# Output projection of an HGRN2 encoder layer by Strassen's seven products instead of eight

## The chip, the cores and the metric

The kernel runs on one core of one Trainium2 chip. The metric is the device time of one execution in microseconds (us). The core has five engines that run their own instruction rows side by side: PE (TensorE, matrix products; its weight loads are shown apart as PEld), DVE (VectorE), ACT (ScalarE), POOL (GpSimd) and SP (SyncE), which here does nothing but issue DMA transfers, in the order of its row. An engine works its row off in order; an instruction that waits holds up all that stand behind it.

## The reference

One layer on two sequences, a prompt of 1024 tokens and a sample of 256, with a model width of 1024, 16 heads of 128 and a mixer width of 2048. Cut to what the kernel computes:

```python
h = _rms(x) * norm_g * (1.0 + scale) + shift
q, f_fw, f_bw, i, z = jnp.split(h @ w_in, 5, axis=-1)
o = gated_chunkwise(q, k_fw, i, g_fw) + flip(gated_chunkwise(flip(q), flip(k_bw), flip(i), flip(g_bw)))
o = (_rms(o) * norm_g_head).reshape(B, L, 2048)
y = (o * jax.nn.silu(z)) @ w_out          # 2048 -> 1024
x = x + gate * y
return _rms(x) * final_g
```

The last three lines are the stage that is changed. Below, u stands for `o * silu(z)`, a matrix of 1280 tokens by 2048, and w_out has 2048 rows and 1024 columns.

## The kernel before

All 1280 tokens are worked as ten blocks of 128 (`NT = 10`; blocks 0 to 7 are the prompt, 8 and 9 the sample). The program has two stages. In the long first one PE projects h for the 16 heads and, in between, runs the attention of the heads. When a head is done, `norm` multiplies its output by the head norm and writes u for that head to a buffer in HBM: heads 0 to 14 into `u_dram`, head 15 into `u_last`. It does this for three stretches of tokens; the last one, `norm(2)` of head 15, comes at the very end of the attention, and it is called late (`held`). The second stage, from about 1460 us on, is the output projection.

Products are made in float32 accuracy out of a faster format: each operand is split into a high part (a cast on ACT) and a low part (the raw value minus the high part, on DVE or POOL), and a product is three matmuls, high by high, high by low, low by high. `load_wo(pl, e)` does that for 128 rows of w_out, `load_u(j, half)` for one token block and one half of the 2048 columns of u. Both fetch a raw tile (`wraw`, `ur`, three buffers each) by a DMA that SP issues. `y_mm` issues the three matmuls for one token block j, one half n of the output columns (512) and one e; 16 e's with three matmuls each fill one PSUM bank, so the projection has 10 x 2 x 16 x 3 = 960 matmuls of 128 by 128 by 512.

`y_ahead` runs 96 of these matmuls while the last pieces of the attention are still coming; `piece(todo)` puts these pieces between them. After `norm(2)` the rest follows, block by block. When the two banks of a block are full, DVE multiplies by the gate row and adds x, ACT sums the squares, and DVE scales by the final norm and `final_g`; SP writes the result. The pool `pa` of buffers is opened when the first stage's weights are given back, the pool `pb` when the attention's are.

What sets the order: PE's row is in the order of the code (`manual_schedule`). For the other engines the framework's scheduler orders the instructions by readiness and priority (`high_priority` moves a group forward), so the order of a row of ACT, DVE, POOL or SP is not that of the code; it is fixed when the program is built. PSUM's eight banks are shared by four groups of names: pj (3), sc (2), ob (1), tu (2).

Of the kernel before, what the change touches and what calls it, by code (L numbers as in the profile page):

```python
# [19 lines left out]
P = 128  # L20
D = 1024
# [24 lines left out]
def kernel(  # L46
# [29 lines left out]
    u_dram = dram.tile([P, NH - 1, T], F32, name="u_dram")  # L76
    u_last = dram.tile([P, 1, T], F32, name="u_last")
# [428 lines left out]
    def attention(e):  # L506
# [117 lines left out]
        def norm(si):  # L624
# [11 lines left out]
            dst = u_dram[:, e, s0:s0 + sl] if e < NH - 1 else u_last[:, 0, s0:s0 + sl]  # L636
            sp.dma_start(dst, u)
# [15 lines left out]

    HALF = NH // 2
    wo_h, wo_l, ub, y_acc = {}, {}, {}, {}

    def load_wo(pl, e):
        wo_h[e] = pl.tile([P, D], F32R, name=f"wo_h{e}")
        wo_l[e] = pl.tile([P, D], F32R, name=f"wo_l{e}")
        raw = pa.tile([P, D], F32, tag="wraw", bufs=3, name=f"wo{e}_r")  # L660
        sp.dma_start(raw, hg_w_out[0, e * P:(e + 1) * P, :])
        act.copy(wo_h[e], raw)
        (pool if e % 2 == 0 and e < HALF or e % 4 == 3 and e >= HALF else dve).tensor_tensor(wo_l[e], raw, wo_h[e].bitcast(F32), ALU.subtract)

    def load_u(j, half):
        pl, bufs = (pb, 2) if half else (pa, 3)
        ur = pa.tile([P, HALF, P], F32, tag="ur", bufs=3, name=f"ur{j}_{half}")
        uh = pl.tile([P, HALF, P], F32R, tag="uh", bufs=bufs, name=f"uh{j}_{half}")
        ul = pl.tile([P, HALF, P], F32R, tag="ul", bufs=bufs, name=f"ul{j}_{half}")
        c = slice(j * P, (j + 1) * P)  # L670
        if half:
            sp.dma_start(ur[:, :HALF - 1], u_dram[:, HALF:, c])
            sp.dma_start(ur[:, HALF - 1:], u_last[:, :, c])
        else:
            sp.dma_start(ur, u_dram[:, :HALF, c])
        act.copy(uh, ur)
        dve.tensor_tensor(ul, ur, uh.bitcast(F32), ALU.subtract)
        ub[j, half] = (uh, ul)
# [4 lines left out]
    def y_bank(j, n):  # L683
        if (j, n) not in y_acc:
            tag = y_tags[(2 * j + n) % 8]
            y_acc[j, n] = ps.tile([P, 512], F32, tag=tag, bufs=y_bufs[tag], name=f"y{j}_{n}")
        return y_acc[j, n]

    def y_mm(j, ns, e):
        uh, ul = ub[j, e // HALF]  # L690
        for u, w, first, last in ((uh, wo_h, True, False), (uh, wo_l, False, False), (ul, wo_h, False, True)):
            for n in ns:
                pe.matmul(y_bank(j, n), u[:, e % HALF, :], w[e][:, n * 512:(n + 1) * 512],  # L693
                          start=first and e == 0, stop=last and e == NH - 1)

    def y_ahead():
        for e in range(HALF):
            for j, n in ((0, 0), (0, 1), (1, 0)):
                y_mm(j, (n,), e)
                yield 0.65  # L700

    with tc.manual_schedule(engines={PE}):
# [80 lines left out]
        for e in range(HALF):  # L783
            y_mm(3, (0, 1), e)
        for j in range(NT):
            if j in FIRST:
                sp.dma_start(gb, gate_dram[FIRST.index(j), :].partition_broadcast(P))
            xj = pa.tile([P, D], F32, tag="wraw", bufs=3, name=f"xj2_{j}")
            sp.dma_start(xj, xs[j])
            if 0 < j and j + 3 < NT:  # L790
                load_u(j + 3, 0)
            if j == 0:
                for e in range(HALF, NH):
                    y_mm(0, (0, 1), e)
                    y_mm(1, (0, 1), e)
            elif j == NT - 1:
                for n in range(2):
                    for e in range(NH):
                        y_mm(j, (n,), e)
            elif j > 1:  # L800
                for e in range(HALF if j < 4 else 0, NH):
                    y_mm(j, (0, 1), e)
            if j + 2 < NT:
                load_u(j + 2, 1)
# [44 lines left out]
```

## Time and profile before

| | |
|---|---|
| median of 3 runs | 1700.11 us (1698.76 to 1700.37) |
| the profiled execution | 1697.91 us, its span 1696.2 us |
| granted TensorE clock, mean | 0.995 |
| PE busy | 1649.5 us, 97% of the span |
| DVE busy | 988.6 us, 58% |
| ACT busy | 822.3 us, 48% |
| POOL busy | 638.4 us, 38% |

The span is the time from the first to the last instruction that the profiler saw; all rows of the trace count from its start. A busy share is a mean over the whole span, which hides that the stages differ. A granted clock of 1.0 is 2.4 GHz, 0.5 is 1.2 GHz.

### The profile page before, as it was taken

What the parts mean: (1) busy time and instruction counts of PE and PEld (TensorE: products, weight loads), DVE (VectorE), ACT (ScalarE), POOL (GpSimd) and SP (SyncE); (2) the same over time, 40 slices, a digit from 0 to 9 for tenths busy, and PEclk for the clock granted to TensorE, in tenths of its full rate; (3) what the DMA queues carried; (4) which work ended last, traced back from release to release, by engine and by line L of the source; (5) the groups of instructions that cost most, each with busy time, mean ns of one, the idle gap of its engine ahead of it and who ended that gap; (6) DMA issues with size and microseconds to landing.
All of it is one profiled execution on the core that took longest, in us unless ns stands there. A gap on an engine that the chain in (4) does not pass through costs nothing.

```text
span 1696.2 us, 28353 instructions
## 1 busy us (share of the span) xinstructions
PE 1649.5 (97%) x11511; PEld 1438.9 (85%) x11511; DVE 988.6 (58%) x2127; ACT 822.3 (48%) x1261; POOL 638.4 (38%) x595
## 2 busy tenths in 40 slices
PE   5999999999999999999999999999999999899998
PEld 4798789888988898889888988889888988788886
DVE  5646565657566755764477448644865477834322
ACT  6543634464546454645455545643573457542210
POOL 1533434353345343444354434534444344510000
PEclk8999999999999999999999999999999999999999
DMA  8312311111011011111111110111111100664310
GB/s 283 123 42 61 103 29 40 39 38 39 28 54 38 29 38 41 32 48 38 38 35 47 34 43 29 41 38 43 37 38 35 44 17 13 208 202 144 124 50 25
DMA packets 121268, 103.06 MB, mean 61 GB/s; under 512 B 3929, under 2 KB 108466, under 8 KB 121138
## 3 DMA queue, kind: packets, MB, share of 16 engines
q1 hardware_dynamic: 121138, 101.26, 19.1%
q8 instruction: 90, 1.47, 0.4%
q14 instruction: 40, 0.33, 0.1%
HBM read 85.50 MB, written 15.74 MB: 60 GB/s over the span
## 4 chain that ended last, share of the span: by engine, by line
PE 79%; DVE 9%; ACT 4%; issue 1%; POOL 1%; DMA 0%; DVEq 0%; SPq 0%; POOLq 0%
PE pv L444 14%; PE y L693 13%; PE pff L422 13%; PE pfb L422 13%; PE pq L422 8%; PE pz L422 7%; DVE g L467 4%; PE ob L609 3%; PE up L532 3%; PE sc L553 3%; DVE kts L523 1%; PE kt L520 1%; DVE ku L474 1%; PE sc L559 1%; DVE qe L473 1%
## 5 line engine op out<-in xcount | busy, mean ns | idle before, releaser
L444 PE MATMUL pv<-wv_h,h_hi 128*128 128x256 f32 x640 | 181.2, 283 | 0.0
L444 PE MATMUL pv<-wv_h,h_lo 128*128 128x256 f32 x640 | 181.1, 283 | 0.0
L444 PE MATMUL pv<-wv_l,h_hi 128*128 128x256 f32 x640 | 181.1, 283 | 0.0
L523 DVE COPY kts<-kt 128x512 f32<-128x512 f32 (+2 forms) x96 | 48.0, 500 | 210.5 <-PE kt L520 210.3
L488 POOL TENSOR_TENSOR ku<-xx,dec 128x256 f32<-128x256 f32 (+1 forms) x96 | 69.6, 725 | 262.6 <-PE up L532 120.1
L422 PE MATMUL pz<-h_hi,wz_h 128*128 128x512 f32 (+1 forms) x384 | 144.4, 376 | 0.0
L422 PE MATMUL pff<-h_hi,wff_h 128*128 128x512 f32 (+1 forms) x360 | 138.5, 385 | 0.0
L422 PE MATMUL pq<-h_hi,wq_h 128*128 128x512 f32 (+1 forms) x360 | 138.1, 384 | 0.0
L422 PE MATMUL pfb<-h_hi,wfb_h 128*128 128x512 f32 (+1 forms) x384 | 136.3, 355 | 0.6 <-DVE q L406 0.6
L422 PE MATMUL pz<-h_hi,wz_l 128*128 128x512 f32 (+1 forms) x384 | 136.7, 356 | 0.0
L422 PE MATMUL pz<-h_lo,wz_h 128*128 128x512 f32 (+1 forms) x384 | 136.4, 355 | 0.0
L422 PE MATMUL pfb<-h_lo,wfb_h 128*128 128x512 f32 (+1 forms) x384 | 136.0, 354 | 0.0
L422 PE MATMUL pfb<-h_hi,wfb_l 128*128 128x512 f32 (+1 forms) x384 | 135.9, 354 | 0.0
L422 PE MATMUL pq<-h_hi,wq_l 128*128 128x512 f32 (+1 forms) x360 | 128.3, 357 | 0.0
L422 PE MATMUL pff<-h_hi,wff_l 128*128 128x512 f32 (+1 forms) x360 | 128.3, 356 | 0.0
L422 PE MATMUL pff<-h_lo,wff_h 128*128 128x512 f32 (+1 forms) x360 | 128.0, 356 | 0.0
L422 PE MATMUL pq<-h_lo,wq_h 128*128 128x512 f32 (+1 forms) x360 | 128.0, 355 | 0.0
L444 PEld LDWEIGHTS pv<-wv_l,h_hi 128*128 128x128 f32 x640 | 122.9, 192 | 0.0
L444 PEld LDWEIGHTS pv<-wv_h,h_lo 128*128 128x128 f32 x640 | 122.9, 192 | 0.0
L444 PEld LDWEIGHTS pv<-wv_h,h_hi 128*128 128x128 f32 x640 | 122.9, 192 | 0.0
L397 POOL TENSOR_SCALAR k<-g,k_scale,k_bias 128x512 f32<-128x512 f32 (+1 forms) x96 | 68.0, 708 | 141.0 <-ACT g L395 141.0
L467 DVE TENSOR_TENSOR_SCAN g<-reset,g 128x512 f32<-128x512 uint8 (+1 forms) x96 | 105.8, 1121 | 20.2 <-ACT g L459 20.2
(198 smaller groups left out, 4536.0 us busy)
## 6 DMA issues: line engine op xcount, KB each, us to landing
xj<-in_x_prompt_dram SPq DMA_DIRECT2D x16, 512.0 KB
wq_r<-in_hg_w_in_dram SPq DMA_DIRECT2D x16, 512.0 KB
aw<-in_ada_w_dram SPq DMA_DIRECT2D x16, 512.0 KB
wff_r<-in_hg_w_in_dram SPq DMA_DIRECT2D x16, 512.0 KB
wv_r<-in_hg_w_in_dram SPq DMA_DIRECT2D x16, 512.0 KB
wfb_r<-in_hg_w_in_dram SPq DMA_DIRECT2D x16, 512.0 KB
wz_r<-in_hg_w_in_dram SPq DMA_DIRECT2D x16, 512.0 KB
wo_r<-in_hg_w_out_dram SPq DMA_DIRECT2D x16, 512.0 KB
```

The source lines that it names most:

```text
L397: pool.tensor_scalar(k, g, k_scale[:, e:e + 1], k_bias[:, e:e + 1], ALU.mult, ALU.add)
L422: pe.matmul(acc[:, :sl], a[:, k, :], h[si][:, k, :], start=n == 0, stop=n == 3 * KT - 1)
L444: pe.matmul(acc[:, :2 * P], h[si][:, k, c], a[:, k % 4, :], start=n == 0, stop=n == 3 * KT - 1)
L467: dve.tensor_tensor_scan(gs, reset[:, :sl], gs, 0.0, ALU.mult, ALU.add)
L473: dve.tensor_tensor(chunks(qe), g3, g3[:, :, mid:mid + 1].broadcast_to([P, nch, C]), ALU.subtract)
L474: dve.tensor_tensor(chunks(ku), g3[:, :, last:last + 1].broadcast_to([P, nch, C]), g3, ALU.subtract)
L488: pool.tensor_tensor(u4[:, :, ca], x4[:, :, ca], dec[:, :, cb].broadcast_to([P, nb, C]), ALU.mult)
L523: dve.tensor_copy(kt[:, c], tp[:, c])
L532: pe.matmul(up[:, c], kt[:, c], v_t[e, b], start=True, stop=True)
L553: pe.matmul(sps[d][c * C:(c + 1) * C, i, c * C:(c + 1) * C], ke[:, o:o + C], qe[:, o:o + C], start=True, stop=True)
L609: pe.matmul(ob[:, c], l, r, start=n == 0, stop=n == len(ops) - 1)
L693: pe.matmul(y_bank(j, n), u[:, e % HALF, :], w[e][:, n * 512:(n + 1) * 512], start=first and e == 0, stop=last and e == NH - 1)
```

## The change

The product of u (1280 by 2048) and w_out (2048 by 1024) is cut into two by two blocks: the tokens into blocks 0 to 4 and 5 to 9, the 2048 into heads 0 to 7 and 8 to 15, the output columns into two halves of 512. Strassen's scheme makes the four output blocks from seven products of such half-size blocks in place of eight; for that, sums and differences of blocks of u and of w_out are formed first, and sums and differences of products afterwards. The products are called M1, M7, M5, M6, M4, M3 and M2, in the order in which they run. Each runs over five pairs of token blocks (block p and block p + 5 are a pair); one product on one pair is a unit, 24 matmuls into one bank, and there are 35 units, the five of a product in a row.

`prep_w(m)` makes the eight high and low weight tiles (`bh`, `bl`, 128 by 512) of product m; it is called at the start of the product before. Raw tiles of w_out come through a ring of three buffers of one name (`wr`; the second operands, called `ws` in M7, are in the same ring), and for M7, M5, M6 and M4 POOL subtracts two of them, or one from a running tile `t0` to `t7`, before the split. All low parts of weights are made on POOL. `prep_u(m, p)` does the same for u, two units ahead of use, with the sums and low parts on DVE; the tiles are `uh` and `ul`, three of each, and the raw ones `ur` and `us`. `collect` takes a bank when it is full: M1, M7 and M5 are copied to SBUF by ACT, the four others are combined by DVE as they come, and the output's gate, x, squares and final norm are worked on half a row at a time (`half`, `gate`, `square`, `final`, not shown). The buffer of u in HBM is laid out anew, so that a token block of eight heads is contiguous in each partition; a head's write now has pieces of 128 tokens, 512 bytes. All of the remaining attention, `norm(2)` of head 15 with it, now comes after M1's five units.

```diff
-    u_dram = dram.tile([P, NH - 1, T], F32, name="u_dram")
-    u_last = dram.tile([P, 1, T], F32, name="u_last")
+    u_dram = [dram.tile([P, NT, NH // 2, P], F32, name="u_a"),
+              dram.tile([P, NT, NH // 2 - 1, P], F32, name="u_b")]
+    u_last = dram.tile([P, NT, 1, P], F32, name="u_last")
...
-            dst = u_dram[:, e, s0:s0 + sl] if e < NH - 1 else u_last[:, 0, s0:s0 + sl]
-            sp.dma_start(dst, u)
+            bl = slice(s0 // P, (s0 + sl) // P)
+            dst = u_dram[e // HALF][:, bl, e % HALF] if e < NH - 1 else u_last[:, bl, 0]
+            sp.dma_start(dst, u.rearrange("p (b c) -> p b c", c=P))
...
+    PAIRS = NT // 2
+    W = D // 2
+    pools = {}
+    wk, uk, xacc, trow, srow = {}, {}, {}, {}, {}
+    def load_b(t, i, j, k):
+        sp.dma_start(t, hg_w_out[0, (i * HALF + k) * P:(i * HALF + k + 1) * P, j * W:(j + 1) * W])
+    def raw_b(i, j, k, name):
+        t = pools["a"].tile([P, W], F32, tag="wr", bufs=3, name=name)
+        load_b(t, i, j, k)
+        return t
+    def prep_w(m):
+        for k in range(HALF):
+            if m in (1, 3, 2):
+                t = raw_b(*{1: (0, 0), 3: (1, 1), 2: (1, 0)}[m], k, f"wr{m}_{k}")
+            elif m == 7:
+                t = raw_b(1, 1, k, f"wr{m}_{k}")
+                t2 = raw_b(0, 1, k, f"ws{m}_{k}")
+                pool.tensor_tensor(t, t, t2, ALU.subtract)
+            elif m == 5:
+                t = trow[k] = pools["b"].tile([P, W], F32, name=f"t{k}")
+                load_b(t, 0, 1, k)
+                t2 = raw_b(0, 0, k, f"wr{m}_{k}")
+                pool.tensor_tensor(t, t, t2, ALU.subtract)
+            elif m == 6:
+                t = trow[k]
+                t2 = raw_b(1, 1, k, f"wr{m}_{k}")
+                pool.tensor_tensor(t, t2, t, ALU.subtract)
+            else:
+                t = trow[k]
+                t2 = raw_b(1, 0, k, f"wr{m}_{k}")
+                pool.tensor_tensor(t, t, t2, ALU.subtract)
+            hi = pools["a"].tile([P, W], F32R, tag="bh", bufs=2 * HALF, name=f"bh{m}_{k}")
+            lo = pools["a"].tile([P, W], F32R, tag="bl", bufs=2 * HALF, name=f"bl{m}_{k}")
+            act.copy(hi, t)
+            pool.tensor_tensor(lo, t, hi.bitcast(F32), ALU.subtract)
+            wk[m, k] = (hi, lo)
+    def load_a(t, i, j, p):
+        b = i * PAIRS + p
+        if j == 0:
+            sp.dma_start(t, u_dram[0][:, b])
         else:
+            sp.dma_start(t[:, :HALF - 1], u_dram[1][:, b])
+            sp.dma_start(t[:, HALF - 1:], u_last[:, b])
+    def raw_a(i, j, p, name):
+        first = "b" not in pools
+        t = pools["a" if first else "b"].tile([P, HALF, P], F32, tag="ur", bufs=2 if first else 3, name=name)
+        load_a(t, i, j, p)
+        return t
+    def prep_u(m, p):
+        if m in (1, 4, 2):
+            t = raw_a(*{1: (0, 0), 4: (1, 1), 2: (0, 1)}[m], p, f"ur{m}_{p}")
+        elif m == 7:
+            t = raw_a(1, 0, p, f"ur{m}_{p}")
+            t2 = raw_a(0, 0, p, f"us{m}_{p}")
+            dve.tensor_tensor(t, t2, t, ALU.subtract)
+        elif m == 5:
+            t = srow[p] = pools["b"].tile([P, HALF, P], F32, name=f"s{p}")
+            load_a(t, 1, 1, p)
+            t2 = raw_a(1, 0, p, f"ur{m}_{p}")
+            dve.tensor_tensor(t, t, t2, ALU.add)
+        else:
+            t = srow[p]
+            t2 = raw_a(0, 0 if m == 6 else 1, p, f"ur{m}_{p}")
+            if m == 6:
+                dve.tensor_tensor(t, t, t2, ALU.subtract)
+            else:
+                dve.tensor_tensor(t, t2, t, ALU.subtract)
+        uh = pools["a"].tile([P, HALF, P], F32R, tag="uh", bufs=3, name=f"uh{m}_{p}")
+        ul = pools["a"].tile([P, HALF, P], F32R, tag="ul", bufs=3, name=f"ul{m}_{p}")
+        act.copy(uh, t)
+        dve.tensor_tensor(ul, t, uh.bitcast(F32), ALU.subtract)
+        uk[m, p] = (uh, ul)
...
+    units = [(m, p) for m in (1, 7, 5, 6, 4, 3, 2) for p in range(PAIRS)]
...
+    def collect(m, p, bank):
+        if m in (1, 7, 5):
+            t = xacc[m, p] = pools["a" if m == 1 else "b"].tile([P, W], F32, name=f"x{m}_{p}")
+            act.copy(t, bank)
+            return
+        x1, x7, x5 = (xacc[i, p] for i in (1, 7, 5))
+        j1, j2 = p, PAIRS + p
+        if m == 6:
+            c22 = xacc["c22", p] = pools["b"].tile([P, W], F32, name=f"c22_{p}")
+            u2 = pools["b"].tile([P, W], F32, tag="tmp", bufs=2, name=f"u2_{p}")
+            dve.tensor_tensor(u2, bank, x1, ALU.add)
+            dve.tensor_tensor(x7, x7, u2, ALU.add)
+            dve.tensor_tensor(c22, x7, x5, ALU.add)
+            dve.tensor_tensor(x5, x5, u2, ALU.add)
+            half(j2, 1, c22, bank)
+        elif m == 4:
+            dve.tensor_tensor(x7, x7, bank, ALU.subtract)
+            half(j2, 0, x7, bank)
+            final(j2, (x7, xacc["c22", p]))
+            half(j1, 0, x1, None)
+        elif m == 3:
+            dve.tensor_tensor(x5, x5, bank, ALU.add)
+            half(j1, 1, x5, bank)
+        else:
+            t = pools["b"].tile([P, W], F32, tag="tmp", bufs=2, name=f"c11_{p}")
+            gate(j1, 0, t, bank)
+            dve.tensor_tensor(x1, x1, t, ALU.add)
+            square(j1, 0, x1, bank)
+            final(j1, (x1, x5))
+    def y_unit(i):
+        m, p = units[i]
+        if p == 0 and i + PAIRS < len(units):
+            prep_w(units[i + PAIRS][0])
+        if i + 2 < len(units):
+            prep_u(*units[i + 2])
+        tag = y_tags[(i if m == 1 else i - PAIRS + 3) % 8] if m != 1 else "pj"
+        bank = ps.tile([P, 512], F32, tag=tag, bufs=y_bufs[tag], name=f"y{m}_{p}")
+        uh, ul = uk.pop((m, p))
+        for k in range(HALF):
+            bh, bl = wk[m, k]
+            for n, (u, w) in enumerate(((uh, bh), (uh, bl), (ul, bh))):
+                pe.matmul(bank, u[:, k, :], w, start=k == n == 0, stop=k == HALF - 1 and n == 2)
+            yield 0.65
+        collect(m, p, bank)
...
-        pa = tc.alloc_tile_pool(name="pa", bufs=1, side="right", reuse_waits="tile")
+        pa = pools["a"] = tc.alloc_tile_pool(name="pa", bufs=1, side="right", reuse_waits="tile")
         with tc.high_priority(offset=1500):
-            load_u(0, 0)
-            load_wo(pa, 0)
-        load_wo(pa, 1)
-        load_u(1, 0)
-        for e in range(2, HALF):
-            load_wo(pa, e)
-        load_u(2, 0)
+            prep_u(1, 0)
+            prep_w(1)
+        prep_u(1, 1)
         todo.append(held)
         for _ in range(LEAD):
             piece(todo)
         credit = 0.0
-        for dt in y_ahead():
-            credit += dt
-            if len(todo) > 1 and credit >= PACE_TAIL:
-                piece(todo)
-                credit -= PACE_TAIL
-        while len(todo) > 1:
+        for i in range(PAIRS):
+            for dt in y_unit(i):
+                credit += dt
+                if len(todo) > 1 and credit >= PACE_TAIL:
+                    piece(todo)
+                    credit -= PACE_TAIL
+        while todo:
             piece(todo)
-        for e in range(HALF):
-            y_mm(1, (1,), e)
-        piece(todo)
         pp.release()
-        pb = tc.alloc_tile_pool(name="pb", bufs=1, reuse_waits="tile")
-        for e in range(HALF, NH):
-            load_wo(pb, e)
-        load_u(0, 1)
-        load_u(1, 1)
+        pb = pools["b"] = tc.alloc_tile_pool(name="pb", bufs=1, reuse_waits="tile")
         fg = pb.tile([P, D], F32, name="fg")
         sp.dma_start(fg, final_g.partition_broadcast(P))
-        gb = pb.tile([P, D], F32, name="gb")
-        for e in range(HALF):
-            y_mm(2, (0, 1), e)
-        load_u(3, 0)
-        for e in range(HALF):
-            y_mm(3, (0, 1), e)
...
+        gbs = [pb.tile([P, D], F32, name=f"gb{r}") for r in range(2)]
+        for r in range(2):
+            sp.dma_start(gbs[r], gate_dram[r, :].partition_broadcast(P))
+        for i in range(PAIRS, len(units)):
+            for _ in y_unit(i):
+                pass
         pb.release()
         pa.release()
```

The instruction rows of the engines change as follows. Names carry numbers of the build at their end; `wr7_4` is the raw weight tile 4 of M7. First, SP's row where the weights of M7 are loaded, in the program after the change (there is nothing like it before, where each w_out tile is loaded once):

```order
L672 DMA wr7_3_15046<-in_hg_w_out_dram 128x512
L672 DMA ws7_3_15048<-in_hg_w_out_dram 128x512
L672 DMA wr7_4_15055<-in_hg_w_out_dram 128x512
L640 DMA u_last_65<-z15_1_14752 128x512
L672 DMA ws7_4_15057<-in_hg_w_out_dram 128x512
L672 DMA wr7_5_15064<-in_hg_w_out_dram 128x512
L710 DMA us7_0_15289<-u_a_63 128x1024
L672 DMA ws7_5_15066<-in_hg_w_out_dram 128x512
L672 DMA wr7_6_15073<-in_hg_w_out_dram 128x512
```

Each weight k of M7 has two loads, `wr7_k` and `ws7_k`, in turn, with loads of u (`us7_0`) and a write of u (`z15_1`) between them. Second, POOL's row at the end of the weights of M7 and the start of those of M5, after the change:

```order
L687 TENSOR_TENSOR wr7_5_15064<-wr7_5_15064,ws7_5_15066 128x512
L704 TENSOR_TENSOR bl7_5_15070<-wr7_5_15064,bh7_5_15069 128x512
L687 TENSOR_TENSOR wr7_6_15073<-wr7_6_15073,ws7_6_15075 128x512
L704 TENSOR_TENSOR bl7_6_15079<-wr7_6_15073,bh7_6_15078 128x512
L687 TENSOR_TENSOR wr7_7_15082<-wr7_7_15082,ws7_7_15084 128x512
L704 TENSOR_TENSOR bl7_7_15088<-wr7_7_15082,bh7_7_15087 128x512
L637 TENSOR_TENSOR z15_2_14859<-z15_2_14859,rs15_2_15252 128x256
L692 TENSOR_TENSOR t0_15376<-t0_15376,wr5_0_15378 128x512
L692 TENSOR_TENSOR t1_15385<-t1_15385,wr5_1_15387 128x512
```

Per weight POOL has one subtraction of two raw tiles (L687) and one for the low part (L704). Then comes the last norm's product (`z15_2`), and then M5's running tiles, of which the row holds 16 instructions in all for t0 to t7 (a subtraction and a low part each; the subtraction of t7 is the 15th). Third, SP's row between them, after the change:

```order
L672 DMA wr5_2_15396<-in_hg_w_out_dram 128x512
L640 DMA u_last_65<-z15_2_14859 128x256
L896 DMA fg_15370<-in_final_g_dram 128x1024
L899 DMA gb0_15372<-gate_dram_66 128x1024
L899 DMA gb1_15373<-gate_dram_66 128x1024
L672 DMA t0_15376<-in_hg_w_out_dram 128x512
L672 DMA t1_15385<-in_hg_w_out_dram 128x512
```

The write of the last stretch of u stands ahead of `fg`, of two rows of the gate, which were one row before, and of the running tiles. Last, ACT's row around the last norm of head 15. Before the change:

```order
L676 CAST uh3_0_15348<-ur3_0_15347 128x1024
L633 ACT_TABLE_LOAD
L633 ACTIVATE rs15_2_15163<-ms15_2_15221,eps_t_71 128x256
L634 ACT_TABLE_LOAD
L634 ACTIVATE rs15_2_15163<-rs15_2_15163 128x256
L662 CAST wo_h8_15232<-wo8_r_15234 128x1024
L662 CAST wo_h9_15238<-wo9_r_15240 128x1024
L662 CAST wo_h10_15244<-wo10_r_15246 128x1024
L676 CAST uh0_1_15281<-ur0_1_15280 128x1024
L676 CAST uh1_1_15288<-ur1_1_15287 128x1024
```

The table loads and activations of the norm are followed by casts of the second half's weights and of u. After the change, first at the last norm:

```order
L703 CAST bh7_7_15087<-wr7_7_15082 128x512
L786 COPY x1_4_15357<-y1_4_15332 128x512
L635 ACT_TABLE_LOAD
L635 ACTIVATE rs15_2_15252<-ms15_2_15359,eps_t_72 128x256
L636 ACT_TABLE_LOAD
L636 ACTIVATE rs15_2_15252<-rs15_2_15252 128x256
L786 COPY x7_0_15482<-y7_0_15457 128x512
L786 COPY x7_1_15518<-y7_1_15493 128x512
L703 CAST bh5_0_15381<-t0_15376 128x512
```

and a little further down, where `bh5_1` to `bh5_4` stand between the two pieces:

```order
L703 CAST bh5_5_15426<-t5_15421 128x512
L703 CAST bh5_6_15435<-t6_15430 128x512
L703 CAST bh5_7_15444<-t7_15439 128x512
L743 CAST uh7_2_15453<-ur7_2_15448 128x1024
L743 CAST uh7_3_15489<-ur7_3_15484 128x1024
L786 COPY x7_2_15554<-y7_2_15529 128x512
L743 CAST uh7_4_15525<-ur7_4_15520 128x1024
```

The last cast of M7's weights and the copy of M1's last bank now stand ahead of the norm's table loads, and all eight casts of M5's weights ahead of the casts of u for the third, fourth and fifth unit of M7 (`uh7_2`, `uh7_3`, `uh7_4`).

## Rows read from the trace of the kernel before

**Rows 1.** The page: busy times, DMA share in 40 slices (tenths), chain by engine

```profile
PE 1649.5 (97%) x11511; PEld 1438.9 (85%) x11511; DVE 988.6 (58%) x2127; ACT 822.3 (48%) x1261; POOL 638.4 (38%) x595
...
DMA  8312311111011011111111110111111100664310
...
PE 79%; DVE 9%; ACT 4%; issue 1%; POOL 1%; DMA 0%; DVEq 0%; SPq 0%; POOLq 0%
```

**Rows 2.** Windows: stretch, length, busy PE PEld DVE ACT POOL, clock, DMA, GB/s

```profile
1460.00:1492.00 32.00, 30.23 (x179) 25.29 (x178) 19.23 (x25) 19.00 (x22) 16.86 (x11) 1.00 0.68 213
1492.00:1689.00 197.00, 196.56 (x865) 161.75 (x863) 66.17 (x97) 43.15 (x75) 5.54 (x3) 1.00 0.35 111
1689.00:1697.00 8.00, 0.00 (x0) 0.00 (x0) 2.74 (x6) 1.02 (x3) 0.00 (x0) 0.71 0.17 66
```

**Rows 3.** Timeline of PE: start, length, engine, line, operation, tiles

```profile
1459.99 0.48 PE L693 MATMUL y<-wo_h,uh 128*128 128x512 f32 x1
...
1491.61 0.28 PE L628 MATMUL ms<-sh,ones_r 128*128 128x256 f32 x1
...
1688.19 0.39 PE L693 MATMUL y<-wo_h,ul 128*128 128x512 f32 x1
```

**Rows 4.** Groups of POOL, 1440 to 1697 us: busy time, mean ns of one

```profile
L581 POOL TENSOR_TENSOR aa<-aa,a_bw 128x512 f32<-128x512 f32 x2 | 2.6, 1292 | 4.9 <-DVE a_bw L579 4.9
```

**Rows 5.** Timeline of POOL

```profile
1456.67 5.77 POOL L663 TENSOR_TENSOR wo_l<-wo_r,wo_h 128x1024 fp32r<-128x1024 f32 x2
...
1494.33 0.74 POOL L635 TENSOR_TENSOR z<-z,rs 128x256 f32<-128x256 f32 x1 [5.19 <-ACT rs L634]
```

**Rows 6.** Timelines of SP and of the loads' consumers

```profile
1471.51 0.33 SPq L661 DMA_DIRECT2D wo_r<-in_hg_w_out_dram  x1
1475.27 1.05 ACT L662 CAST wo_h<-wo_r 128x1024 fp32r<-128x1024 f32 x1 [1.99 <-DMA wo_r<-in_hg_w_out_dram]
...
1.26 0.28 SPq L232 DMA_DIRECT2D crow<-in_c_sample_dram  x1
2.85 0.26 PE L244 MATMUL lb_ps<-ident,crow 16*128 16x16 f32 x1 [2.85 <-DMA crow<-in_c_sample_dram]
```

**Rows 7.** Timelines of POOL and DVE, operations that meet

```profile
1473.35 2.39 POOL L663 TENSOR_TENSOR wo_l<-wo_r,wo_h 128x1024 fp32r<-128x1024 f32 x1 [1.86 <-ACT wo_h L662]
1473.75 3.07 DVE L663 TENSOR_TENSOR wo_l<-wo_r,wo_h 128x1024 fp32r<-128x1024 f32 x1
...
1481.26 0.75 DVE L621 SCALAR_TENSOR_TENSOR z<-ob,ng_half,z 128x512 f32<-128x512 f32 x1 [2.98 <-ACT sh L619]
1481.58 1.30 POOL L620 TENSOR_TENSOR sl<-rs,sh 128x512 fp32r<-128x512 f32 x1
```

**Rows 8.** Timeline of DVE in the projection

```profile
1534.02 1.29 DVE L809 TENSOR_TENSOR yt<-y,gb 128x512 f32<-128x512 f32 x2 [9.72 <-PE y L693]
1535.23 1.22 DVE L677 TENSOR_TENSOR ul<-ur,uh 128x1024 fp32r<-128x1024 f32 x1
```

**Rows 9.** Timeline of ACT

```profile
1480.64 0.59 ACT L619 ACTIVATE sh<-ob 128x512 fp32r<-128x512 f32 x1
...
1492.05 0.47 ACT L633 ACTIVATE rs<-ms,eps_t 128x256 f32<-128x256 f32 x1 [2.04 <-PE ms L629]
1492.54 1.28 ACT L634 ACT_TABLE_LOAD   x1
...
1503.59 1.05 ACT L662 CAST wo_h<-wo_r 128x1024 fp32r<-128x1024 f32 x1 [4.60 <-DMA wo_r<-in_hg_w_out_dram]
```

**Rows 10.** Timeline of SP's issues

```profile
1495.54 0.35 SPq L778 DMA_DIRECT2D fg<-in_final_g_dram  x1
...
1496.47 2.60 SPq L661 DMA_DIRECT2D wo_r<-in_hg_w_out_dram  x3
```

**Rows 11.** Windows near the start, columns as in rows 2

```profile
36.00:40.00 4.00, 3.92 (x9) 3.15 (x10) 3.27 (x7) 3.30 (x7) 1.32 (x2) 0.50 1.10 349
40.00:44.00 4.00, 4.00 (x75) 3.56 (x77) 2.79 (x6) 1.96 (x4) 0.00 (x0) 0.97 0.70 225
```

More of the change, by code (lines that the diff above doesn't have):

```diff
@@ L654 @@
     HALF = NH // 2
[L655 to L673, printed above, removed]
-        else:
[L675 to L678, printed above, removed]
+    PAIRS = NT // 2
@@ L680 @@
     y_tags = ("pj", "pj", "pj", "sc", "sc", "ob", "tu", "tu")
     y_bufs = {"pj": 3, "tu": 2, "sc": 2, "ob": 1}
[L683 to L694, printed above, removed]
@@ L696, in y_ahead, with half @@
-    def y_ahead():
-        for e in range(HALF):
-            for j, n in ((0, 0), (0, 1), (1, 0)):
-                y_mm(j, (n,), e)
-                yield 0.65
+    units = [(m, p) for m in (1, 7, 5, 6, 4, 3, 2) for p in range(PAIRS)]
+    def half(j, n, t, bank):
+        c = slice(n * W, (n + 1) * W)
+        gate(j, n, t)
+        xj = pools["b"].tile([P, W], F32, tag="xh", bufs=4, name=f"xh{j}_{n}")
+        sp.dma_start(xj, xs[j][:, c])
+        dve.tensor_tensor(t, t, xj, ALU.add)
+        if bank is not None:
+            square(j, n, t, bank)
@@ new lines, in gate, with square, final @@
+    def gate(j, n, t, src=None):
+        gb = gbs[0 if j < FIRST[1] else 1]
+        dve.tensor_tensor(t, t if src is None else src, gb[:, n * W:(n + 1) * W], ALU.mult)
+    def square(j, n, t, bank):
+        if j not in ssums:
+            ssums[j] = pools["b"].tile([P, 2], F32, tag="ssum2", bufs=NT, name=f"ssum2_{j}")
+        act.activation(bank, t, AF.Square, accum_out=ssums[j][:, n:n + 1])
+    def final(j, ts):
+        rst = pools["b"].tile([P, 1], F32, tag="rst2", bufs=2, name=f"rst2_{j}")
+        dve.tensor_tensor(rst, ssums[j][:, 0:1], ssums[j][:, 1:2], ALU.add)
+        act.activation(rst, rst, AF.Sqrt, bias=eps_t, scale=1.0 / D)
+        dve.reciprocal(rst, rst)
+        for n, t in enumerate(ts):
+            c = slice(n * W, (n + 1) * W)
+            dve.scalar_tensor_tensor(t, t, rst, fg[:, c], ALU.mult, ALU.mult)
+            sp.dma_start(ys[j][:, c], t)
@@ new lines @@
+    ssums = {}
+    def collect(m, p, bank):
[27 more added lines that the diff above has]
+            final(j1, (x1, x5))
@@ L782 @@
-        load_u(3, 0)
-        for e in range(HALF):
-            y_mm(3, (0, 1), e)
[L785 to L804, printed above, removed]
-            yt = pb.tile([P, D], F32, tag="yt", bufs=1, name=f"yt{j}")
-            ssum = pb.tile([P, 2], F32, tag="ssum2", bufs=2, name=f"ssum2_{j}")
-            for n in range(2):
-                c = slice(n * 512, (n + 1) * 512)
-                dve.tensor_tensor(yt[:, c], y_bank(j, n), gb[:, c], ALU.mult)
-                dve.tensor_tensor(yt[:, c], yt[:, c], xj[:, c], ALU.add)
-                act.activation(y_bank(j, n), yt[:, c], AF.Square, accum_out=ssum[:, n:n + 1])
-            rst = pb.tile([P, 1], F32, tag="rst2", bufs=2, name=f"rst2_{j}")
-            dve.tensor_tensor(rst, ssum[:, 0:1], ssum[:, 1:2], ALU.add)
-            act.activation(rst, rst, AF.Sqrt, bias=eps_t, scale=1.0 / D)
-            dve.reciprocal(rst, rst)
-            for n in range(2):
-                c = slice(n * 512, (n + 1) * 512)
-                dve.scalar_tensor_tensor(yt[:, c], yt[:, c], rst, fg[:, c], ALU.mult, ALU.mult)
-                sp.dma_start(ys[j][:, c], yt[:, c])
```

## Prediction

> **What bounds the kernel now.** I read the page first: TensorE (PE) is busy 97% of the span and holds 79% of the chain that ended last, so only what shortens PE's row of work, or makes it wait, can move the time [rows 1]. Then the windows of the stage that the change rewrites. From 1492 to 1689 us PE is busy 196.56 of 197 us while POOL works 5.54 us in all, DVE a third and ACT a fifth of the time [rows 2]: the projection runs at PE's own pace with three nearly empty engines beside it. After PE's end there are 8 us in which DVE and ACT finish the last block. The timeline of PE gives the pace: the first y matmul starts at 1459.99, the first of the two matmuls of the last norm stands at 1491.61, the last y matmul starts at 1688.19 [rows 3]. Of the 960 y matmuls 96 lie ahead of that norm and 864 behind it, so one costs 196.6 / 864 = 0.2275 us.
>
> **What is removed.** Seven products of five pairs of 24 matmuls are 840, not 960: 120 x 0.2275 = 27.3 us less PE work. That is the whole possible gain, 1.6%. A unit of 24 matmuls (one product, one pair, one PSUM bank) lasts 5.46 us, a product 27.3 us. PE has no other saving to offer, so the question is whether the operands are there every 5.46 us.
>
> **What is added, engine by engine.** Weights are no longer split once and kept: each product makes its own eight hi/lo pairs of 128x512, four of the seven with a subtraction ahead, all on POOL. That is 56 + 32 = 88 POOL operations, at 1.29 us for a 128x512 of two tensors [rows 4] 113 us, where a handful of operations stood before. The loads of w_out grow from 8 to 18 MB, those of u from 10 to 22.5 MB.
>
> The place that decides is M7, the second product. Follow POOL's row. In the kernel before it reaches its first weight at 1456.67 [rows 5]; I take 1456 for the new one. Eight lo parts of M1 and three operations of the attention, 11 x 1.29, end at 1470; the second load of M7's first weight lands about a microsecond later, so the first subtraction starts at 1471. From here on each of M7's eight weights needs two raw tiles out of a ring of three, and by the order of SP and POOL the second tile of weight k+1 is loaded into the buffer that the subtraction of weight k frees. So subtraction, issue, load and subtraction follow each other. A 512 KB load issued alone at 1471.51 is consumed at 1475.27, 3.76 us; a tiny one issued at 1.26 at 2.85, 1.59 us [rows 6]. A 256 KB load lies between, halfway 2.7 us. One weight then takes 1.29 + 0.1 + 2.7 = 4.1 us, eight take 7 x 4.1 + 1.3 = 30. Five 512 KB u loads stand between them in SP's queue, 0.7 us each: 3.5. DVE prepares u at the same time, and there the trace shows something else: a DVE subtraction of 128x1024 that takes 1.22 us alone [rows 8] took 3.07 us when it started at 1473.75 beside a POOL operation that ran to 1475.74; it ended 1.08 us after that [rows 7]. The two did not overlap. A DVE operation with one operand in PSUM (1481.26, 0.75 us) passed beside POOL at its usual length [rows 7]. For seven such DVE operations in this stretch I add 3 us. The last subtraction of M7 ends at 1471 + 30 + 3.5 + 3 = 1507.5.
>
> Behind it on ACT stand the cast, a copy of M1's last bank and two table loads with the last norm's activations, 0.6 + 0.6 + 2 x 1.28 + 2 x 0.47 = 4.7 us [rows 9], then POOL's product of 0.74 us [rows 5]: 1513. Only then does SP issue the write of the last u, then fg, the two gate rows and t0. In the trace fg was issued at 1495.54, then a gate row and three w_out tiles, and the first of these, the third 512 KB in a row, was consumed at 1503.59, 8.05 us after fg's issue [rows 9, 10]. With one more 256 KB, 8.9 us from 1513.5: t0 is there at 1522.4.
>
> Now ACT's order, shown above: the eight casts of M5's weights stand ahead of uh7_2, the operand of M7's *third* unit, and the last of them needs POOL's last subtraction, 15 operations after t0 lands: 15 x 1.29 = 19.4. From the fourth weight on a cast of 0.6 us plus a hand-over lies between its two POOL operations, 4 x 0.7 = 2.8. Then 0.6 for that cast and 1.05 for uh7_2's own [rows 9]: 23.8 us. **uh7_2 is ready at 1546.** PE wants it much earlier: M1's 120 matmuls, 27.3 us, and the attention between them, 8.4 us (the 30.23 us of PE in the 32 after 1460 [rows 2] less 96 y matmuls), end at about 1496, and at 1503 with the waits that POOL's late norm operands cost there (they do not count, PE waits later anyway); two units of M7 later it is 1514. So PE stands still for some 32 us, more than the whole gain, and the time follows from 1546, not from PE's past.
>
> From 1546 on 28 units remain, 28 x 5.46 = 153 us. Further waits:
> - *M7's fifth and M5's third unit.* uh5_2 stands on ACT behind all casts of M6's weights, whose buffers come free in M7's last unit. From there 11 POOL operations, 14.3 us, against 16.4 us of PE work that covers them; but three of the loads behind them are issued only after DVE has worked off earlier u tiles. I take 1 + 6 us; 0 if the loads are early, 8 if DVE's subtractions each push POOL.
> - *M3.* Between the first combination of M6 and ul3_2 DVE's row has 13 operations of 1.22 us, 63 of 0.65 (as the pairs of 1.29) and 8 small ones [rows 8]: 58 us, from 5.5 us after M6's start, where PE needs ul3_2 65.5 us after it. Alone that just fits. About 18 POOL operations of 1.29 us (lo parts for M4, M3 and M2) fall among them, and if each pushes an operation, as in rows 7, DVE is up to 23 us late. Nothing: 0; all: 23. I take 11, nearer to the measured full exclusion less what falls into PSUM operations and gaps.
> - *Clock.* PE stopped at 1688.6, and over the next 8 us the granted clock averaged 0.71 [rows 2, 3]; near the start it was 0.50 (1.2 GHz) from 36 to 40 us with PE busy and 0.97 in the next four [rows 11]. After waits of 32, 6 and 11 us some microseconds go at half pace: 3 us (0 to 6).
>
> The end is as before: 1696.2 - 1688.6 = 7.6 us. Moving nothing else, the 512-byte pieces in which u is now written fall where the DMA share is one to three tenths, from the third slice of the page to the 33rd [rows 1]: 0.
>
> **Sum.** 1546 + 153 + 7 + 11 + 3 + 7.6 = 1727.6 us of span against 1696.2: +31.4. The profiled run took 1697.91, 1.7 us more than its span; the median of the runs shown is 1700.11, 2.2 above it. So 1729 by the profiled run, 1731 by the median; I say 1730.
>
> The exclusion has a page in the Trainium skill. "SBUF — State Buffer", section "SBUF: two separate sides", says that GpSimd and a VectorE instruction with two SBUF inputs share a port pair under an exclusive lock, held for the whole instruction. By that rule all 18 operations in M6 to M3 would count, 12 us more than I took, and the span would be 1740. The trace agrees in the one case shown (3.07 us, against 0.75 us unhindered with an operand in PSUM).
>
> **Bounds.** With loads of 1.6 us and no pushing, uh7_2 is ready at 1534; with loads of 3.76 us at 1555, and with POOL slowed by DVE as well 1560. Later waits together 1 to 38. Extremes: 1696 and 1758 of span.
>
> **Rivals.**
> - *Faster: the preparation keeps up.* POOL's operations up to uh7_2 are 42 long and 3 short ones, 56 us from 1456: 1512 without any wait, less than PE's 1514. Then only M3 waits: 1697.9 - 27.3 + 0 to 11 = 1671 to 1682. For it speaks that the engines were nearly empty [rows 2]; against it the ring of three, the table loads and ACT's order. The point that decides: uh7_2's time and the later waits must together stay under 1696.2 - 7.6 - 153 = 1535.6. Chance 0.09, with all of its mixtures (1671 to 1694).
> - *Even:* loads near the low bound and DVE never pushed, 1695 to 1704. Chance 0.06; about 0.04 of it within 0.2%, 3.4 us, which is about what a measurement of this kernel can tell from no change.
> - *Worse: POOL and DVE exclude each other everywhere.* M7's and M5's chains and M6 to M3 all take the upper bounds: 1752 to 1770. Chance 0.13.
> - *Forecast:* M7's third unit waits 20 to 40 us, later ones 7 to 30: 1704 to 1752, likeliest 1730. Chance 0.72.
>
> That the change does not do what it says is excluded: in the programs' orders PE's row has 8973 entries instead of 9093, 120 fewer. Faster 0.09 + 0.01, same 0.04, slower 0.86. The range 1704 to 1752 leaves out the first, the third and most of the second.
>
> **What would show it.** In the new profile: y matmuls 840 at the same spacing; one gap of PE of 20 to 40 us that ends with ACT's uh cast of M7's third unit; M7's POOL subtractions about 4 us apart, each behind its second load; SP's fg at about 1513; DVE's subtractions at 2 to 3 us where POOL works; small waits for ul in M3. Wrong would be the forecast if that gap were under 10 us, because loads land within 2 us or because the casts of M5 are done when PE gets there.

## The result and the profile after

The changed kernel takes 1746.89 us (median of 4 runs, 1745.56 to 1748.42) against 1700.24 us in the same session: ratio 1.0276, interval 1.0263 to 1.0289, 47 us slower. The forecast was 1730 with a range to 1752. The profiled execution has a span of 1744.2 us.

The page after: busy times, to be held against [rows 1].

```profile
PE 1640.3 (94%) x11391; PEld 1426.5 (82%) x11391; DVE 1073.3 (62%) x2192; ACT 861.4 (49%) x1331; POOL 759.2 (44%) x677
```

TensorE has 120 matmuls fewer, POOL 121 us more work, and the span is 48 us longer: TensorE stands still. Its timeline shows where (start, length, what it did, in brackets the idle time ahead and what ended it); the first row is the last matmul ahead of the long wait:

```profile
1520.40 0.39 PE L825 MATMUL y<-bh,ul 128*128 128x512 f32 x1
1551.33 0.80 PE L825 MATMUL y<-bh,uh 128*128 128x512 f32 x1 [30.54 <-ACT uh L743]
...
1586.99 0.80 PE L825 MATMUL y<-bh,uh 128*128 128x512 f32 x1 [5.50 <-ACT uh L743]
...
1592.86 0.40 PE L825 MATMUL y<-bh,ul 128*128 128x512 f32 x1
...
1651.92 0.80 PE L825 MATMUL y<-bh,ul 128*128 128x512 f32 x1 [6.27 <-DVE ul L744]
...
1686.54 0.79 PE L825 MATMUL y<-bh,uh 128*128 128x512 f32 x1 [4.41 <-ACT uh L743]
1692.29 0.79 PE L825 MATMUL y<-bh,ul 128*128 128x512 f32 x1 [4.53 <-DVE ul L744]
...
1736.58 0.39 PE L825 MATMUL y<-bh,ul 128*128 128x512 f32 x1
```

Counting the y matmuls, 24 to a unit, puts the waits at M7's third unit (1551), M5's third (1587), M4's third (1652) and M3's third (1687 and 1692). It is the third unit each time: the operands of a product's first two units are prepared during the product before, those of the third are the first that the program calls behind all weights of the next.

The long wait, followed backwards, on ACT (the cast of M5's last weight, then uh7_2), POOL (the first and the last subtraction of M7's weights, the last norm's product, the first and the last subtraction of M5's) and SP (the load of the final norm's row):

```profile
1549.71 0.62 ACT L703 CAST bh<-t 128x512 fp32r<-128x512 f32 x1 [3.12 <-POOL t L692]
1550.24 1.04 ACT L743 CAST uh<-ur 128x1024 fp32r<-128x1024 f32 x1
...
1475.20 1.29 POOL L687 TENSOR_TENSOR wr<-wr,ws 128x512 f32<-128x512 f32 x1 [1.89 <-DMA ws<-in_hg_w_out_dram]
...
1510.19 2.31 POOL L687 TENSOR_TENSOR wr<-wr,ws 128x512 f32<-128x512 f32 x1 [2.34 <-DMA ws<-in_hg_w_out_dram]
...
1517.24 0.74 POOL L637 TENSOR_TENSOR z<-z,rs 128x256 f32<-128x256 f32 x1 [2.73 <-ACT rs L636]
1527.71 2.48 POOL L692 TENSOR_TENSOR t<-t,wr 128x512 f32<-128x512 f32 x2 [9.73 <-DMA t<-in_hg_w_out_dram]
...
1548.42 1.25 POOL L692 TENSOR_TENSOR t<-t,wr 128x512 f32<-128x512 f32 x1
...
1518.38 0.43 SPq L896 DMA_DIRECT2D fg<-in_final_g_dram  x1
```

uh7_2's cast follows M5's eighth without a gap. Its own operand was ready, but only just: SP's row, too, has M5's weights ahead of us7_2, the second raw tile of that operand. It is issued at 1540.40, and DVE's sum waits for it until 1546.12 and ends at 1547.3, 2.9 us before the cast starts (SP, then DVE):

```profile
1540.40 0.42 SPq L710 DMA_DIRECT2D us<-u_a  x1
...
1546.12 1.22 DVE L728 TENSOR_TENSOR ur<-us,ur 128x1024 f32<-128x1024 f32 x1 [34.75 <-DMA us<-u_a]
```

So a change on ACT's row alone could win some 3 us here; that is an estimate from these rows. The eighth cast waits for POOL, POOL for t0, t0 for the row and the two gate rows ahead of it on SP, these for the last norm's write, and so back to M7's first subtraction at 1475.

Windows of the long wait and of the two restarts (length, busy PE, PEld, DVE, ACT, POOL, granted clock, DMA share, GB/s):

```profile
1520.00:1551.00 31.00, 0.79 (x4) 0.33 (x2) 1.22 (x1) 6.20 (x10) 19.65 (x16) 0.57 0.74 248
1551.00:1556.00 5.00, 4.41 (x11) 3.08 (x12) 3.58 (x3) 1.32 (x2) 0.67 (x1) 0.58 0.53 166
1586.00:1593.00 7.00, 5.26 (x12) 3.72 (x13) 4.87 (x4) 2.47 (x3) 1.82 (x2) 0.52 0.28 73
```

POOL is busy two thirds of the wait, DVE 1.2 of 31 us. Behind both waits TensorE runs for some microseconds near the lower level of its clock, 1.2 GHz (0.58 and 0.52 granted).

From the last matmul of the last norm (1508.3) to the last y matmul (1736.6) there are 720 y matmuls, 163.8 us at 0.2275 us each. What is left is waits (the sum of the brackets) and a rest: the slower clock behind waits, and stalls too short for a bracket. For the changed kernel: 228.3 = 163.8 + 53.6 + 10.9. Other kernels are split in the same way below.

### The profile page after: what moved, and what is told of

Read it like the earlier page. It is cut to its first block, busy times and chain, and to the rows that moved or that the text cites. A ratio compares the mean times of both kernels' runs of the same rounds, so it can differ in the third digit from the quotient of the medians.

```text
span 1744.2 us, 28586 instructions
## 1 busy us (share of the span) xinstructions
PE 1640.3 (94%) x11391; PEld 1426.5 (82%) x11391; DVE 1073.3 (62%) x2192; ACT 861.4 (49%) x1331; POOL 759.2 (44%) x677
## 5 line engine op out<-in xcount | busy, mean ns | idle before, releaser
L825 PE MATMUL y<-bh,uh 128*128 128x512 f32 x280 | 115.1, 411 | 40.5 <-ACT uh L743 40.5
L825 PE MATMUL y<-bh,ul 128*128 128x512 f32 x280 | 113.9, 407 | 12.3 <-DVE ul L744 12.3
```

What stands on the lines that cost most here:

```text
L825: pe.matmul(bank, u[:, k, :], w, start=k == n == 0, stop=k == HALF - 1 and n == 2)
```

## The experiments

Times are ratios to the kernel before, run beside each; the changed kernel is 1.0276.

**One cause at a time.** First, operands of M7's units ahead of M5's weights. The edit moves their loads on SP, their sums on DVE and their casts on ACT together:

```diff
+        if i == PAIRS:
+            for k in (2, 3, 4):
+                prep_u(*units[i + k])
         if p == 0 and i + PAIRS < len(units):
             prep_w(units[i + PAIRS][0])
-        if i + 2 < len(units):
+        if i + 2 < len(units) and i not in (PAIRS, PAIRS + 1, PAIRS + 2):
             prep_u(*units[i + 2])
```

> Only the order of preparation changes: at the first unit of M7 the operands of its units 2, 3 and 4 are prepared ahead of M5's weights, so that on ACT uh7_2 no longer stands behind all eight casts of M5's weights. Theory (ACT's row order holds uh7_2 back while M5's weights are made): uh7_2 is ready at about 1532 us, the 30.5 us wait of TensorE falls to about 12, M7 ends near 1551 instead of 1570, M5's weights are just ready then, and the time falls by about 16 us, to 1731 (1724 to 1738). Rival (the queue of loads is the bound, order only moves the wait): TensorE waits as long in all, at M5's first unit instead, and the time falls by less than 5 us.

1739.28 us, 1.0234 (1.0219 to 1.0249): 7 us, between the two. The wait fell as said, and a second appeared at M5's first unit:

```profile
1530.61 0.80 PE L828 MATMUL y<-bh,uh 128*128 128x512 f32 x1 [10.93 <-ACT uh L743]
...
1558.61 0.80 PE L828 MATMUL y<-bh,uh 128*128 128x512 f32 x1 [8.13 <-ACT uh L743]
```

At M7's third unit it is now the load of us7_2 that ends last:

```profile
1528.25 1.23 DVE L728 TENSOR_TENSOR ur<-us,ur 128x1024 f32<-128x1024 f32 x1 [17.95 <-DMA us<-u_a]
```

At M5's first, uh5_0 stands behind M5's last cast, which ended at 1557.1. The row order is a cause, but behind it the loads and POOL's pace wait. The waits fell by 11 us in all, and the rest rose by 6 (split: 223.5 = 163.8 + 42.5 + 17.2): there were more waits, and behind the longer ones the matmuls came 0.43 us apart, at half pace, again.

Second, the 16 subtractions of M7's and M5's raw weights from `pool.tensor_tensor` to `dve.tensor_tensor`:

> The 16 subtractions of raw weights of M7 and M5 go from POOL to DVE, which is nearly idle from 1511 to 1546 us. Theory (POOL's row, two operations a weight, is half of the chain that makes uh7_2 late): M7's weights come every 4.2 us instead of 5.0, M5's every 2.5 instead of 3.2, uh7_2 is ready 8 to 10 us earlier, the time falls by about 9 us, to 1738 (1734 to 1742). Rival (the loads set the pace, POOL only fills the time between them): 0 to 3 us.

1735.92 us, 1.0217 (1.0198 to 1.0236): 10 us, as the theory had it. The third unit started at 1538.26 after 18.79 us. POOL's length is a cause. What ends last there is again the load of us7_2 (TensorE, then DVE):

```profile
1538.26 0.80 PE L825 MATMUL y<-bh,uh 128*128 128x512 f32 x1 [18.79 <-ACT uh L743]
...
1535.90 1.23 DVE L728 TENSOR_TENSOR ur<-us,ur 128x1024 f32<-128x1024 f32 x1 [3.40 <-DMA us<-u_a]
```

Third, the loads of `fg` and both `gb` issued at `i == 2 * PAIRS + 2` instead of ahead of the loop:

> The loads of the final norm's row and of the two gate rows are issued in M5's third unit instead of ahead of M5's running tiles. Theory (every load ahead of t0 on SP's queue delays uh7_2 one for one): t0 lands about 6 us earlier, 1.5 MB less at the 8 to 9 us that four loads took, uh7_2 comes 6 us earlier, and the time falls by 5 to 6 us, to 1741. Rival (t0 is held by M7's weights or by the write of the last u, not by these loads): no change.

1742.72 us, 1.0254 (1.0239 to 1.0270): 4 us. The third unit started at 1545.10 instead of 1551.33; 6 us at the place as the theory had it, but 4 at the end instead of 5 to 6.

Fourth, for M4, M3 and M2: `(dve if m in (4, 3, 2) else pool).tensor_tensor(lo, t, hi.bitcast(F32), ALU.subtract)`.

> The 24 low parts of the weights of M4, M3 and M2 go from POOL to DVE, so that from M6 on POOL has little to do. Theory (DVE is late in M4 and M3 because POOL and DVE shut each other out while both have two operands in SBUF): DVE gets 24 x 0.65 = 15.6 us more work and loses some 24 us of lengthening, so the waits for ul and uh in M4 and M3, 15.4 us, fall by 6 to 10 us, and the time by as much, to 1739. Rival (DVE simply has too much work there, POOL doesn't matter): the waits grow by up to 15 us, to 1755 or more.

1737.89 us, 1.0228 (1.0211 to 1.0245): 8 us. More work on the engine that is late made it less late. TensorE's waits from 1600 us on are 7.1 us now, 15.4 before:

```profile
PE y L825 <- ACT uh L743: 5.2, 2, 3.7
PE y L825 <- DVE ul L744: 1.9, 3, 1.2
```

The changed kernel's rows in M6 show why, DVE first, then the eight POOL operations beside it, which end at 1625.09:

```profile
1616.46 0.68 DVE L793 TENSOR_TENSOR u<-y,x 128x512 f32<-128x512 f32 x1
...
1620.41 1.79 DVE L795 TENSOR_TENSOR c<-x,x 128x512 f32<-128x512 f32 x1
...
1626.27 0.69 DVE L757 TENSOR_TENSOR c<-c,xh 128x512 f32<-128x512 f32 x1
...
1609.66 15.43 POOL L704 TENSOR_TENSOR bl<-t,bh 128x512 fp32r<-128x512 f32 x8
```

One operation with the bank as an operand is not touched, one on two SBUF tiles takes 1.1 us longer, and POOL's take 1.93 us each instead of 1.29 [rows 4].

**What the sums cost.** In `prep_w` and `prep_u` every second load and every sum left out:

> The seven products in the same order, but no sums of operands: each product takes one raw tile of w_out and one of u, so that the 32 subtractions of weights, the 20 sums of u and their second loads are left out (the output is not that of the projection). Theory (two things cost the time: the sums, and the order of ACT's row, which still puts uh7_2 behind all casts of M5's weights, with DVE's many operations in M4 and M3): the wait at M7's third unit falls from 30 us to about 15, those of M5 vanish, those of M4 and M3 fall to some 9, and the time is about 1704 (1694 to 1714), still no gain. Rival (the sums alone are the cost): without them the 27 us of TensorE's work show in full, 1673 to 1685.

1705.06 us, 1.0032 (1.0018 to 1.0045). Without any sum the changed program still loses to the old one: 10.7 us at M7's third unit and 8.4 us for ul in M7, M4 and M3.

**The rearranged kernel.** The core of its edits (not shown: the 32 subtractions on DVE, the late loads of `fg` and of the second gate row, and the ring of the x tiles `xh`, which has two buffers instead of four):

```diff
-    units = [(m, p) for m in (1, 7, 5, 6, 4, 3, 2) for p in range(PAIRS)]
+    units = [(m, p) for m in (1, 2, 7, 5, 6, 4, 3) for p in range(PAIRS)]
...
-        if p == 0 and i + PAIRS < len(units):
-            prep_w(units[i + PAIRS][0])
         if i + 2 < len(units):
             prep_u(*units[i + 2])
+        if i < PAIRS:
+            if p == 0:
+                prep_w(units[i + PAIRS][0], range(HALF))
+        elif p < 4 and i - p + PAIRS < len(units):
+            prep_w(units[i - p + PAIRS][0], (2 * p, 2 * p + 1))
...
+            (dve if m in (6, 4, 3) else pool).tensor_tensor(lo, t, hi.bitcast(F32), ALU.subtract)
...
+        if m == 2:
+            t = xacc["c11", p] = pools["b"].tile([P, W], F32, name=f"c11_{p}")
+            dve.tensor_tensor(t, bank, xacc[1, p], ALU.add)
+            half(p, 0, t, bank)
+            return
```

> The whole projection, rearranged by what the first four runs showed: M2, which needs no sums, comes second (order M1, M2, M7, M5, M6, M4, M3), weights are prepared two at a time behind the operands of the unit two ahead, all 32 subtractions of weights and the low parts of M6's, M4's and M3's weights are on DVE, the final norm's row is loaded late. Theory (order of the rows, POOL's length and the exclusion of POOL and DVE each cost their share, and they add up): M7's weights have a whole product's time more, the waits fall to 20 to 30 us in all, spread over many units, and the time is 1700 to 1716, about level with the kernel before. Rival (the loads are what is short: 46 MB in 200 us): TensorE waits for loads in nearly every unit of M7 and M5, and the time stays above 1720.

1694.37 us, 0.9969 (0.9958 to 0.9981): faster than the kernel before, and better than the theory's 1700. One bracket of size is left, and the windows behind it hold TensorE full while the loads run at 302 and 341 GB/s; the rival on loads falls.

```profile
1522.78 0.80 PE L827 MATMUL y<-bh,uh 128*128 128x512 f32 x1 [6.03 <-ACT uh L743]
...
1530.00:1560.00 30.00, 30.00 (x134) 24.84 (x133) 23.60 (x25) 11.58 (x20) 9.43 (x7) 1.00 0.90 302
1560.00:1590.00 30.00, 30.00 (x134) 24.88 (x133) 26.45 (x28) 13.99 (x21) 6.82 (x5) 1.00 0.92 341
```

The same program without sums, and with POOL keeping M6's low parts:

> The rearranged program without any sum of operands (as in the run without sums, 32 subtractions of weights, 20 sums of u and their loads left out, the output is not that of the projection), with the subtractions of low parts of M4 and M3 on DVE. It says what 840 matmuls are worth when little else is asked of the other engines. Theory (TensorE's row can be followed, nothing but operand preparation stands against the 27 us): one wait of about 10 us at the third unit of M2, few others, the time about 1690 (1680 to 1698). Rival (the outputs' work on DVE, gate, x and norm in half rows, is itself too much): waits in M6 to M3 remain, 1700 or more.

1689.15 us, 0.9937 (0.9921 to 0.9954). So the sums with their loads cost 41 us in the changed kernel (1.0276 less 1.0032) and about 5 here (0.9969 less 0.9937; M6's low parts on POOL go into this difference too).

Its two halves apart. The order of the products alone (with the ring of two and the late loads):

> Of the rearrangement only the order of the products (M1, M2, M7, M5, M6, M4, M3, with M2's sum made at once and the late load of the final norm's row that goes with it); POOL keeps all subtractions and low parts, and a product's weights are prepared in one piece ahead of the operands of its third unit. Theory (order of the rows and POOL's length are causes of their own): the same knot moves one product on, uh7_2 now waits behind M5's eight casts, which POOL feeds one per 3.2 us from the end of M2 on, the wait is some 15 us instead of 30, those of M4 and M3 stay, and the time is about 1732 (1720 to 1742). Rival (the late start of M7's weights was the cause): with 27 us more the waits in M7 and M5 vanish, 1705 to 1715.

1740.75 us, 1.0244 (1.0229 to 1.0260), 5 us better than the changed kernel. The knot moved on, as expected, and M2's third unit got one too, which I had not seen (uh2_2 comes from the pool that opens only after the attention):

```profile
1528.32 0.80 PE L824 MATMUL y<-bh,uh 128*128 128x512 f32 x1 [12.19 <-ACT uh L743]
...
1576.01 0.79 PE L824 MATMUL y<-bh,uh 128*128 128x512 f32 x1 [16.66 <-ACT uh L743]
```

All but the order:

> The rearrangement without the new order of products (M7 is second again, M2 last): weights two at a time behind the operands of the unit two ahead, all 32 subtractions and the low parts of M6, M4 and M3 on DVE, gate and norm rows loaded late. Theory (M2 second gives the preparation a start; without it the operands of M7's first units are late): waits of 10 to 15 us around M7's first and third units, few later, the time about 1706 (1699 to 1714). Rival (the start matters little, the interleaving and DVE do it all): within 4 us of the rearranged kernel's 1694.

1708.67 us, 1.0053 (1.0039 to 1.0067), 38 us better than the changed kernel. The waits were small and many, 18.6 us behind the norm, none above 3.3, not one long one at M7; the size was right, the place not.

Then the raw tiles of u for M2 from the first pool, `first = name[2] in "12"`:

> The rearranged kernel with one edit: the raw tiles of u for M2 come from the pool that is open from the start, so that uh2_2 no longer waits for the attention's buffers to be given back. Theory: its wait of 6.0 us at M2's third unit and the slower clock behind it go, the time falls by 6 to 8 us to 1687 (1684 to 1691). Rival (the next thing, M7's weights, is as late): 0 to 3 us.

1690.71 us, 0.9951 (0.9939 to 0.9964). The 6.03 us wait is gone, but M7's first unit now waits 3.0 us for M7's last weight (1.63 for its high part, 1.37 for its low part). The gain of 3 us (0.9969 less 0.9951) is half of the expected one, and the intervals overlap.

```profile
1542.75 0.49 PE L827 MATMUL y<-bh,uh 128*128 128x512 f32 x1 [1.63 <-ACT bh L703]
1544.61 0.80 PE L827 MATMUL y<-bl,uh 128*128 128x512 f32 x1 [1.37 <-POOL bl L704]
```

Last, M1's low parts of every second weight on DVE (`m == 1 and k % 2`), on top of that:

> The second rearranged kernel with one edit: the low parts of every second weight of M1 are made on DVE instead of POOL, as the kernel before did with its weights. Theory (between 1455 and 1490 us POOL's eight low parts of M1 and DVE's attention work shut each other out, which makes TensorE wait for the attention's operands, 3 us at 1460 and 2 at 1490, and slows its clock): 2 to 5 us faster, 1687 (1685 to 1690). Rival (DVE is full there too, 0.65 us operations only move the wait): 0, or 2 us slower.

1691.96 us, 0.9952 (0.9939 to 0.9966): nothing, the rival. TensorE's wait for DVE at 1460 grew from 3.04 to 4.47 us.

**The layout alone**, with the old projection:

> The kernel before with one part of the change: u laid out in HBM by token block, so that writes have pieces of 512 bytes and a block of eight heads is contiguous when it is read. The projection is the old one. Theory (the layout costs nothing, its writes lie under a nearly idle DMA): within 2 us of the kernel before. Rival (short pieces delay the first stage or the loads): 3 us or more slower.

1699.84 us, 0.9994 (0.9985 to 1.0003): no difference.

## Why the forecast held, and which terms were off

The mechanism was the one forecast: TensorE's 27.3 us are saved, and a standstill at M7's third unit takes more back. By the prediction's steps, in the profiled execution:

| step | forecast | measured |
|---|---|---|
| M7's first subtraction | 1471 | 1475.2 |
| from it to the end of the last | 36.5 | 37.3 |
| from there to fg's issue | 6 | 5.9 |
| from fg's issue to t0's first use | 8.9 | 9.3 |
| from there to the end of t7's subtraction | 22.2 | 22.0 |
| uh7_2's first matmul | 1546 | 1551.3 |
| waits in M7 and M5 behind it | 7 | 6.8 |
| waits in M4 and M3 | 11 | 15.4 |
| slower clock and small stalls | 3 | 10.4 |
| from TensorE's end on | 7.6 | 7.2 |

The chain through POOL, SP and ACT held within 1 us a step. Its start was 4 us late, and 3 of them are POOL's: the eleven operations ahead took from 1456.69 to 1473.32, 16.6 us instead of 14.2, and ended 3 us after the forecast's 1470. M7's second tile then came 1.9 us after POOL was free, not 1 (4.3 us after its issue at 1470.86). In the second row the agreement is partly luck: five operations of the attention on POOL, 5.3 us, stand between M7's subtractions and in no term of the sum, and no row gives the 0.7 us that I took for each load of u there. The rows sum to the 16.6 us by which the span exceeds the forecast (5.3 + 4.4 - 0.2 + 7.4 - 0.4 = 16.5).

*The clock* is the term most under-sized. I took 3 us for all waits together, and the rest in the split from 1551 on is 185.3 - 671 x 0.2275 - 22.2 = 10.4. By the starts of the matmuls, less 0.2275 us each and less the brackets, 9.4 of it lie directly behind five waits: 1.95 us behind the one of 30.54, 2.59 behind 5.50, 2.70 behind 6.27, and 2.15 behind the two of 4.41 and 4.53 together. The short stalls are the small remainder. I had named the waits of the clock term rightly and priced them at a third.

*POOL against DVE.* The waits in M4 and M3 came to 15.4 us, between the 11 I took and the 23 for full exclusion. With POOL's low parts of M4, M3 and M2 given to DVE 7.1 of them were left, so the exclusion is shown for about 8; how the 7.1 divide between the exclusion that was left and DVE's own load, which that run made larger, is not shown. By the Trainium skill, "SBUF — State Buffer", section "SBUF: two separate sides", a VectorE instruction with two SBUF inputs and a GpSimd instruction that reads SBUF share a port pair, and whichever starts first holds it for the whole instruction; the trace agrees, 1.79 us beside POOL against 0.69 alone for such operations and 0.68 with a PSUM operand. I placed the whole of the wait in M3. It begins in M6 and comes due at M4's third unit already.

*The faster rival* (the preparation keeps up, 1671 to 1682, chance 0.09) was wrong for this program, but what stood against it can be moved: with order, engines and pace changed the kernel is faster than before. It does not reach 1671: in the second rearranged kernel TensorE ends at 1681.6, 20.3 us behind 1688.6 less 27.3. Of that 9.6 lie behind the last norm (173.3 = 163.8 + 6.5 + 3.1). The other 10.7 lie ahead of it: its last matmul runs at 1507.9, in the kernel before at 1491.7, and only 24 x 0.2275 = 5.5 of the difference is work. Most of it is there before M1 starts: the first y matmul starts at 1468.07, in the kernel before at 1459.99. No matmul ahead of the last norm waits for a weight of M1; from 1455 on the waits are for the attention's operands from DVE, ACT and POOL, 6.2 us in four. What makes these late was not tried. The comparison is also a few microseconds too harsh: this profile is of the slowest of five executions (1693.27 us, median 1690.71), the one before, 1697.91 us, lies under all three runs of its session (1698.76 to 1700.37).

What stays open: how the saved time divides among the edits. Alone, the four edits brought 7, 10, 4 and 8 us and the order 5; the whole brought 52, of which all but the order brought 38, so that the same order was worth 14 on top of the rest. They remove waits that stand one behind the other, so no single run prices them. The forecast's worse rival, 1752 to 1770, reaches above its own extreme of 1758 us of span; nothing hangs on it.

## What to carry to other kernels

A product saved on the busiest engine is worth what the other engines leave of it: write down, for each unit, when its last operand is cast, by each engine's own row, before counting the saving. In a row worked in order, preparation for the next stage must not stand ahead of the next unit's operands; interleave it in portions of a unit (interleaving was run only together with the other edits). Look at SP's row as well as at that of the engine that casts: the load that stood behind all of M5's weights was ready for its sum only shortly before the cast that stood behind them. When two engines shut each other out, try giving the work to the faster one, even if it is the one that is late: it paid in M4 and M3 (8 us) and brought nothing at M1.

## What I had not expected of the hardware

The waits of 30.54, 5.50 and 6.27 us each cost 2 to 2.7 us more than their own length, the longest no more than the others, so for the short ones that is up to half as much again. Behind the one of 5.50 us 11 matmuls took from 1586.99 to 1592.86, 5.87 us, 0.75 of it a further wait; at 0.2275 they are 2.5, so 2.6 us went to the clock, granted at 0.52 over the window shown. The rate of the loads, 302 and 341 GB/s at DMA shares of 0.90 and 0.92 in the rearranged kernel, did not hold TensorE up; while it waited in the changed kernel they ran at 248, and a load that came late there did so by its place in SP's row.
